# Seven quarter products for the gate and up matrices of two feed-forward layers

## The chip, the cores and the metric

The kernel runs on one core of a Trainium2 chip. The metric is device time in microseconds (us) of one execution, as the median of repeated runs. All data are float32 in memory. TensorE (PE) multiplies in a 32-bit format called fp32r, so each operand is kept as a high part (rounded to fp32r) and a low part (the rest, rounded again), and a product is made of three matmuls: high by high, high by low, low by high.

## The reference

One encoder block over 512 tokens of 1024 features:

```python
h = h + 0.5 * _swiglu(_rmsnorm(h, ffn1_norm), ffn1_w_in, ffn1_w_out)
z = _rmsnorm(h, mix_norm) @ w_in          # conv, q, k, v, r, gate
...                                       
h = h + concat([y_conv, y_gla]) @ w_out
h = h + 0.5 * _swiglu(_rmsnorm(h, ffn2_norm), ffn2_w_in, ffn2_w_out)
gate = sigmoid(_rmsnorm(h, ple_norm) @ ple_w_gate)
h = h + gate * (p @ ple_w_proj)
return _rmsnorm(h, final_norm)

def _swiglu(x, w_in, w_out):
    gate, up = jnp.split(x @ w_in, 2, axis=-1)   # 1024 -> 2816 each
    return (jax.nn.silu(gate) * up) @ w_out      # 2816 -> 1024
```

The two feed-forward layers (FFN1, FFN2) hold most of the work. Their product with `w_in` is what the change rewrites.

## The kernel before, in words

The residual is kept with features on partitions and tokens along the free axis: eight tiles `hT` of 128 features x 512 tokens. `gsplit` (L163) makes the multiplied operand `hg` from it: gain times h, as a high part (ACT) and a low part (DVE). The factor of the RMS norm, one number per token, is spread over partitions into `rsb` and multiplied in after the product.

A weight tile is fetched by `load` (L171) on SP's queue into the ring `wr` (two buffers of 128 x 2048 floats). `high` (L178) rounds it on ACT into `wh`, `low` (L188) takes the difference on DVE into `wl`; six buffers each. A block of 128 output features is made by `zblock` (L241): for each of eight k tiles of 128 input features three matmuls of 128 x 128 by 128 x 512 into one PSUM bank. PSUM has seven banks named `ps` and one named `ax`.

`ffn` (L454) walks over cuts of the 22 feature blocks (FFN1: 8, 8, 6; FFN2: 12, 10). In a cut it takes the blocks two at a time, here called a pair: gate block, up block, gate block, up block, each a `zblock`. DVE multiplies each result by `rsb`, ACT takes the silu, DVE the product, and `split` (L154) makes its high and low part (`actH`, `actL`). After a cut come its output products: for each of the eight output blocks the matmuls over the cut's feature blocks, then one DVE operation that adds half of the result to h. With the last cut the next operand and the sum of squares (`Norm`, L295) are made as well. Within `ffn`, after its first pair, the order on the engines is left to the planner (`in_order(False)`, L478); elsewhere `Ordered` (L36) keeps PE, DVE and ACT in the order in which the code is written.

The projection (from L572) begins with two weight pairs made ahead in FFN1 (`ahead`, L221), blocks pb0, pa0, pb1, pa1; the column sums of the norm stand inside pb0, the spread of the factor inside pa0 (L579, L593). The convolution's 31 taps run on DVE between the blocks (`taps`, L541), and its layer norm comes shortly before the output product (L957 to L988). The embedding stage (L1045 on) has tokens on the output partitions and ends in two half-wide products of 256 columns (L1062).

PE instructions go through the one helper of L46, so groups are told apart by tiles, not by lines.

Of the kernel before, what the change touches and what calls it, by code (L numbers as in the profile page):

```python
# [15 lines left out]
P = 128  # L16
# [15 lines left out]
FFN1_CUTS = ((0, 8), (8, 16), (16, 22))  # L32
FFN2_CUTS = ((0, 12), (12, 22))
# [29 lines left out]
def block_kernel(ctx: ExitStack, tc: tile.TileContext, a: dict, out: bass.AP):  # L63
    nc = tc.nc
    pe, dve, act = (Ordered(tc, e) for e in (nc.tensor, nc.vector, nc.scalar))
    pool = nc.gpsimd
# [50 lines left out]
    def columns(names, n, tile_name, queue):  # L117

        row = cp.tile([n, P], F32, name=tile_name + "r")
        col = cp.tile([P, n], F32, name=tile_name)  # L120
        r0 = 0
        for name, m in names:
            queue.dma_start(out=row[r0:r0 + m, :], in_=a[name][0].rearrange("(r p) -> r p", p=P))
            for c in range(m):
                vcols[name, c] = col[:, r0 + c:r0 + c + 1]
            r0 += m

        def turn():
            ps = bank()
# [32 lines left out]

    def gsplit(src, g, s):  # L163
# [6 lines left out]

    def load(src, k0, nk, c0, ncol):  # L171
        raw = wp.tile([P, 2048], F32, tag="raw", bufs=2, name=nm("wr"))
        r3 = raw[:, :nk * ncol].rearrange("p (k c) -> p k c", k=nk)
        nc.sync.dma_start(out=r3, in_=src[k0 * P:(k0 + nk) * P, c0:c0 + ncol]
                          .rearrange("(k p) c -> p k c", p=P))
        return r3
# [11 lines left out]
    def low(w):  # L188
        h3, l3, r3 = w
        dve.tensor_tensor(out=l3, in0=r3, in1=h3.bitcast(F32), op=ALU.subtract)  # L190
        return h3, l3
# [29 lines left out]
    def ahead(src, c0, ncol):  # L221


        r3 = load(src, 0, DC, c0, ncol)
        return [[low(w) for w in high4(r3[:, :, c:c + P])] for c in range(0, ncol, P)]
# [41 lines left out]
    def spread(col, copy=True):  # L267
# [7 lines left out]
        bc = tmp("bc", bufs=3)  # L275
# [59 lines left out]
    def square_x(i):  # L335
        for t in range(TB):
            junk = tmp("sq")[:, 0:X_CUTS[i + 1] - X_CUTS[i]]
            act.activation(junk, xt[t][i], AF.Square, accum_out=ssx[:, 4 * t + i:4 * t + i + 1])

    def halves(c0):  # L340

        r3 = wp.tile([P, 2048], F32, tag="raw", bufs=2, name=nm("wr"))[:, 0:D].rearrange("p (k c) -> p k c", k=DC)
        for k in range(0, DC, 4):
            def go(k=k):
                nc.sync.dma_start(out=r3[:, k:k + 4], in_=ffn1_in[k * P:(k + 4) * P, c0:c0 + P]
                                  .rearrange("(k p) c -> p k c", p=P))
# [51 lines left out]
    take(pu0, wu0, range(4, DC))  # L398
    square_x(0)
    early = (parts(raw_g1), parts(raw_u1))  # L400
# [4 lines left out]
    square_x(2)  # L405


    def load_constants():
        act.on, act.last = True, act.latest
        turn = columns(vecs[1:], nrow, "vcol", act)  # L410
        cwrow = bt(s="cwrow")[0:WIDTH, :]
        act.dma_start(out=cwrow, in_=a["conv_w"][0])
        gwu = cp.tile([2 * RANK, 2 * P], F32, name="gwu")
        for i in range(2):
            act.dma_start(out=gwu[i * RANK:(i + 1) * RANK, :], in_=a["gate_w_up"][0])
        act.on = False
        made.extend([turn, cwrow, gwu])

    def constants():
        turn, cwrow, gwu = made  # L420
        turn()
        cw = cp.tile([P, 4 * WIDTH], F32, name="cw")
        ps = bank()
# [5 lines left out]
        m1 = cp.tile([P, 4, CH], F32, name="m1")  # L429
        m2 = cp.tile([P, 4, CH], F32, name="m2")  # L430
# [14 lines left out]
    made = []  # L445

    def first_rows():
        ss = tmp("cs", 16)[:, :TB]
        dve.tensor_reduce(out=ss, in_=ssx.rearrange("p (t i) -> p t i", t=TB)[:, :, 0:3],
                          axis=mybir.AxisListType.X, op=ALU.add)  # L450
        dve.on = act.on = False
        return rsqrt_mean(ss, D, TB)

    def ffn(w_in, w_out, hg, rows, gname, cuts, early=None, meanwhile={}):  # L454
        rsb = None
        norm = Norm()
        nhg = []
        for f0, f1 in cuts:
            acts = []
            for f in range(f0, f1, 2):  # L460
                if early is None:
                    wg = weights(w_in, 0, DC, f * P, 2 * P, P)
                    wu = weights(w_in, 0, DC, DFF + f * P, 2 * P, P)
                else:
                    wg, wu = [None, early[0]], [None, early[1]]
                out = [None, None]
                if early is not None:
                    out[0] = pg0, pu0
                    early = None
                for i in range(2):  # L470
                    if out[i] is None:
                        out[i] = zblock(wg[i], hg), zblock(wu[i], hg)
                    if rsb is None:
                        pe.on, mid = True, []
                        out[1] = zblock(wg[1], hg), zblock(wu[1], hg, {
                            1: lambda: mid.append(rows()), 7: lambda: mid.append(spread(mid[0]))})
                        rsb = mid[1]
                        in_order(False)  # L478
                    pg, pu = out[i]
                    g1 = tmp("g1")  # L480
                    dve.tensor_tensor(out=g1, in0=pg, in1=rsb, op=ALU.mult)
                    s = tmp("s")
                    act.activation(s, g1, AF.Silu)
                    u1 = tmp("u1")
                    dve.tensor_tensor(out=u1, in0=pu, in1=rsb, op=ALU.mult)
                    m = tmp("m")
                    dve.tensor_tensor(out=m, in0=u1, in1=s, op=ALU.mult)
                    acts.append(split(m, "act", cvt if f - f0 < 2 else bt))
                meanwhile.get(f, int)()
            cut = 1 if f1 - f0 <= DC else 2  # L490
            nk = (f1 - f0) // cut
            for n in range(0, DC, 2):
                wa = [weights(w_out, f0 + i * nk, nk, n * P, 2 * P, P) for i in range(cut)]
                for i in range(2):
                    ps = bank()
                    for k in range(f1 - f0):
                        wh, wl = wa[k // nk][i]
                        mm3(ps, wh[:, k % nk, :], wl[:, k % nk, :], *acts[k],
                            k == 0, k == f1 - f0 - 1)
                    h = hT[n + i]  # L500
                    dve.scalar_tensor_tensor(out=h, in0=ps, scalar=0.5, in1=h,
                                             op0=ALU.mult, op1=ALU.add)
                    if f1 == cuts[-1][1]:
                        nhg.append(gsplit(h, vec(gname, n + i), "hg"))
                        norm.add(h)
        return nhg, norm
# [3 lines left out]
    meanwhile = {0: load_constants, 4: constants,  # L510
                 16: lambda: w_ahead.append(ahead(w_in, D_CONV, 2 * P)),
                 18: lambda: w_ahead.append(ahead(w_in, 0, 2 * P))}
    hg, norm = ffn(ffn1_in, a["ffn1_w_out"][0], hg, first_rows, "mix_norm", FFN1_CUTS, early, meanwhile)
# [8 lines left out]
    def pair(c0):  # L522

        r3 = load(w_in, 0, DC, c0, 2 * P)
        return [r3[:, :, i * P:(i + 1) * P] for i in range(2)]
# [53 lines left out]
    pb0 = zblock(wb[0], hg, {6: lambda: mid.append(rsqrt_mean(colsum([norm.acc]), D, TB))})  # L579
# [13 lines left out]
    pa0 = zblock(wa[0], hg, {1: lambda: mid.append(spread(mid[0]))})  # L593
    rs, rsb = mid
    low(w2a[1])
# [3 lines left out]
    pb1 = zblock(wb[1], hg)  # L599
# [45 lines left out]
    raw_v = [load(w_in, 0, 4, C_V, SEQ)]  # L645
# [67 lines left out]
    raw_r = [load(w_in, 0, 4, C_R, SEQ)]  # L713
    wv.append(high(rows4(raw_v, 2)))
# [3 lines left out]
    wv.append(high(rows4(raw_v, 3)))  # L718
# [5 lines left out]
    raw_r.append(load(w_in, 4, 4, C_R, SEQ))  # L724
# [81 lines left out]
    def outputs(t2):  # L806
# [13 lines left out]
        for t in (2 * t2, 2 * t2 + 1):  # L820
            junk = tmp("sq")
# [300 lines left out]
```

## Time and profile before

| what | us |
| --- | --- |
| median of 3 runs | 988.74 (988.57 to 989.16) |
| the profiled execution | 989.85 |
| its span, first to last instruction | 988.1 |
| PE busy in it | 972.3 |
| DVE, ACT busy in it | 533.7, 353.2 |

The span is one execution on the chip by the hardware profiler. A group of instructions is shown with its output and input tiles, shapes, count, busy time, mean length and the idle time before it. The ends of matmuls are modelled and consecutive ones overlap, so a matmul's own length (390 ns at 512 columns) is not what it costs in a row of them: that is the distance of their starts.

### The profile page before, as it was taken

What the parts mean: (1) busy time and instruction counts of PE and PEld (TensorE: products, weight loads), DVE (VectorE), ACT (ScalarE), POOL (GpSimd) and SP (SyncE); (2) the same over time, 40 slices, a digit from 0 to 9 for tenths busy, and PEclk for the clock granted to TensorE, in tenths of its full rate; (3) what the DMA queues carried; (4) which work ended last, traced back from release to release, by engine and by line L of the source; (5) the groups of instructions that cost most, each with busy time, mean ns of one, the idle gap of its engine ahead of it and who ended that gap; (6) DMA issues with size and microseconds to landing.
All of it is one profiled execution on the core that took longest, in us unless ns stands there. A gap on an engine that the chain in (4) does not pass through costs nothing.

```text
span 988.1 us, 11174 instructions
## 1 busy us (share of the span) xinstructions
PE 972.3 (98%) x4570; PEld 800.6 (81%) x4570; DVE 533.7 (54%) x756; ACT 353.2 (36%) x538; POOL 32.2 (3%) x43
## 2 busy tenths in 40 slices
PE   7999999999999999999999999999999999999996
PEld 5888888888888888788877888888888888888885
DVE  4654434444434565999986944443334454355454
ACT  5633222322223343454564633232222232234442
POOL 1000000000000000001220000000000000000000
PEclk9999999999999999999999999999999999999999
DMA  5633222322432331125654332231333222133212
GB/s 162 195 123 117 94 86 89 125 85 86 142 114 75 97 127 42 43 69 145 128 79 122 106 122 86 90 103 64 96 118 128 86 86 95 54 102 114 84 43 86
DMA packets 96505, 98.96 MB, mean 100 GB/s; under 512 B 3284, under 2 KB 89894, under 8 KB 96453
## 3 DMA queue, kind: packets, MB, share of 16 engines
q1 hardware_dynamic: 90592, 93.93, 29.5%
q0 software_dynamic: 5680, 4.20, 3.1%
q8 instruction: 36, 0.59, 0.2%
q14 instruction: 17, 0.13, 0.0%
q10 hardware_dynamic: 180, 0.12, 0.0%
HBM read 92.46 MB, written 2.10 MB: 96 GB/s over the span
## 4 chain that ended last, share of the span: by engine, by line
PE 98%; ACT 0%; DVE 0%; DMA 0%; SPq 0%; issue 0%; POOLq 0%; DVEq 0%; ACTq 0%
PE ps L46 97%; PE ax L46 1%; DMA wr<-in_ffn_w_in 0%; SPq L150 0%; DVE wl L46 0%; ACT yc L46 0%; DVE ygL L46 0%; DVE yc L46 0%; ACT ygH L46 0%; ACT hgH L46 0%; POOLq L1118 0%; ACT ycH L46 0%; ACT wa L46 0%; DVE m L46 0%; ACT h L46 0%
## 5 line engine op out<-in xcount | busy, mean ns | idle before, releaser
L46 ACT CAST wh<-wr 128x1024 fp32r<-128x1024 f32 (+2 forms) x174 | 172.1, 992 | 442.7 <-PE ps L46 419.2
L46 PE MATMUL ps<-hgH,wh 128*128 128x512 f32 x752 | 293.1, 390 | 0.0
L46 PE MATMUL ps<-hgL,wh 128*128 128x512 f32 x752 | 292.6, 389 | 0.0
L46 PE MATMUL ps<-hgH,wl 128*128 128x512 f32 x752 | 292.6, 389 | 0.0
L46 DVE TENSOR_TENSOR wl<-wr,wh 128x1024 fp32r<-128x1024 f32 (+2 forms) x169 | 193.3, 1147 | 61.4 <-ACT wh L46 61.4
L46 PEld LDWEIGHTS ps<-hgH,wh 128*128 128x128 f32 x752 | 141.2, 188 | 29.9 <-issue 0.8
L46 PEld LDWEIGHTS ps<-hgH,wl 128*128 128x128 f32 x752 | 141.1, 188 | 29.5
L46 PEld LDWEIGHTS ps<-hgL,wh 128*128 128x128 f32 x752 | 141.2, 188 | 29.3 <-DVE hgL L46 0.2
L46 PE MATMUL ps<-actL,wh 128*128 128x512 f32 x352 | 137.1, 389 | 0.0
L46 PE MATMUL ps<-actH,wl 128*128 128x512 f32 x352 | 137.0, 389 | 0.0
L46 PE MATMUL ps<-actH,wh 128*128 128x512 f32 x352 | 136.8, 389 | 0.0
L46 DVE TENSOR_TENSOR u<-ps,bc 128x512 f32<-128x512 f32 x48 | 33.1, 690 | 131.9 <-PE ps L46 131.9
L46 DVE SCALAR_TENSOR_TENSOR cv<-glu,cw,cv 128x504 f32<-128x504 f32 (+25 forms) x120 | 81.2, 728 | 0.6
L46 DVE TENSOR_TENSOR g<-ps,bc 128x512 f32<-128x512 f32 x48 | 33.1, 690 | 86.0 <-PE ps L46 83.1
L46 PEld LDWEIGHTS ps<-actL,wh 128*128 128x128 f32 x352 | 66.1, 188 | 14.0 <-DVE actL L46 0.3
L46 PEld LDWEIGHTS ps<-actH,wl 128*128 128x128 f32 x352 | 66.1, 188 | 13.8
L46 PEld LDWEIGHTS ps<-actH,wh 128*128 128x128 f32 x352 | 66.1, 188 | 13.6
L46 DVE SCALAR_TENSOR_TENSOR h<-ps,h 128x512 f32<-128x512 f32 x40 | 27.7, 692 | 88.8 <-PE ps L46 88.7
L46 PE MATMUL ps<-wh,hgH 128*128 128x512 f32 (+1 forms) x136 | 52.4, 385 | 0.0
L46 PE MATMUL ps<-wl,hgH 128*128 128x512 f32 (+1 forms) x136 | 51.7, 380 | 0.0
L46 PE MATMUL ps<-wh,hgL 128*128 128x512 f32 (+1 forms) x136 | 51.3, 377 | 0.0
L46 ACT ACTIVATE s<-g 128x512 f32<-128x512 f32 x48 | 30.3, 632 | 39.9 <-DVE g L46 35.2
(190 smaller groups left out, 767.6 us busy)
## 6 DMA issues: line engine op xcount, KB each, us to landing
wr<-in_ffn_w_in SPq DMA_DIRECT2D x42, 1024.0 KB, 5.1
wr<-in_w_in SPq DMA_DIRECT2D x10, 1024.0 KB, 5.2
wr<-in_ffn_w_out SPq DMA_DIRECT2D x12, 768.0 KB, 4.6
wr<-in_ffn_w_out SPq DMA_DIRECT2D x8, 1024.0 KB, 5.1
wr<-in_ffn_w_out SPq DMA_DIRECT2D x8, 640.0 KB, 4.1
wr<-in_w_out SPq DMA_DIRECT2D x4, 1024.0 KB
wr<-in_ple_w_gate SPq DMA_DIRECT2D x8, 512.0 KB, 3.5
wl<-wr POOLq DMA_DIRECT2D x5, 512.0 KB, 8.7
```

Source lines behind the costliest of these rows:

```text
L46: inst = call(*args, **kwargs)
```

## The change

In both layers the product with `w_in` is made in another way from the fourth pair of blocks on. Take for one pair the 256 gate features and the 256 up features, the 1024 input features in two halves of 512, and the tokens in two halves of 256. The pair's product is then a 2 x 2 by 2 x 2 product of quarters, and it is made with seven products and sums (Winograd's form) in place of eight. Products are named m1 to m7, sums of weights S1 to S4, sums of the normed input t1 to t4. A product runs over four k tiles, two blocks of 128 features and three matmuls of 256 columns. Results that several outputs share stay in a PSUM bank and are added to; ACT takes copies of it on the way (`snap`).

```diff
-FFN1_CUTS = ((0, 8), (8, 16), (16, 22))
-FFN2_CUTS = ((0, 12), (12, 22))
+HALF = SEQ // 2
+CUTS = ((0, 4), (4, 8), (8, 12), (12, 16), (16, 22))
...
+    def raw(nk, ncol):
+        return wp.tile([P, 1024], F32, tag="raw", bufs=6, name=nm("wr"))[:, :nk * ncol].rearrange(
+            "p (k c) -> p k c", k=nk)
...
-        return [[low(w) for w in high4(r3[:, :, c:c + P])] for c in range(0, ncol, P)]
+        return [[low(w, pool) for w in high4(load(src, 0, DC, c, P))] for c in range(c0, c0 + ncol, P)]
...
+    def mul(ps, w, x, first, last, ks=range(4)):
+
+        (wh, wl), k0 = w, ks[0]
+        for k in ks:
+            xh, xl = x[k]
+            for i in range(2):
+                cs = slice(i * P, (i + 1) * P)
+                o = ps[:, i * HALF:(i + 1) * HALF]
+                end = last and k == ks[-1] and i == 1
+                pe.matmul(o, wh[:, k - k0, cs], xh, start=(first and k == ks[0] and i == 0), stop=False, skip_group_check=True)
+                pe.matmul(o, wh[:, k - k0, cs], xl, start=False, stop=False, skip_group_check=True)
+                pe.matmul(o, wl[:, k - k0, cs], xh, start=False, stop=end, skip_group_check=True)
...
+    class Left:
+        def part(self, name, engine=None):
+
+            if name not in self.done:
+                self.done[name] = low(high(getattr(self, name)), engine or dve)
+            return self.done[name]
...
+            self.sum(self.s1, self.a21, self.a22, ALU.add)
+            self.sum(self.s2, self.s1, self.a11)
...
+            self.sum(self.s3, self.a11, self.a21)
...
+            self.sum(self.s4, self.a12, self.s2)
...
+        def m1(p):
+            p.x = bank()
+            mul(p.x, p.part("a11"), x.op["b11"], True, False)
+            p.a = snap(p.x, "sq", bufs=3)
+
+        def m2(p):
+            p.y = bank()
+            mul(p.y, p.part("a12"), x.op["b21"], True, True)
+
+            def gate0():
+                p.s0 = silu(plus(p.y, p.a, 0, "g1"))
+
+            return [gate0]
+
+        def m6(p):
+            mul(p.x, p.part("s2"), x.op["t2"], False, False)
+            p.u2 = snap(p.x, "u2", bufs=1)
+
+        def m7(p):
+            p.w = bank()
+            mul(p.w, p.part("s3"), x.op["t3"], True, False)
+
+        def m5(p):
+            mul(p.x, p.part("s1"), x.op["t1"], False, False)
+            p.u = plus(p.w, snap(p.x, "sq", bufs=3), 1, "u1")
+
+        def m4(p):
+            mul(p.w, p.part("a22"), x.op["t4"], False, True)
+            gated(p, p.s0, plus(p.w, p.u2, 0, "u1"), 0)
+
+        def m3(p):
+            mul(p.x, p.part("s4"), x.op["b22"], False, True)
+            s = silu(times_row(p.x, 1, "g1"))
+            return [lambda: gated(p, s, p.u, 1), lambda: act_parts(p)]
...
+            before = [(AHEAD, lambda: p.part(part))] if part else []
+            if kind in ("m1", "m2"):
+                before.append((7, lambda: p.fetch(part)))
+            elif kind == "m6":
+                before += [(9, lambda: p.fetch("a21", "a22")), (6, p.s12)]
+            elif kind in ("m7", "m3"):
+                before.append((6, p.s3_ if kind == "m7" else p.s4_))
...
+        for i in range(start, npair):
+            add("m6", i)
+            add("m7", i)
+            add("m5", i)
+            if i == end:
+                half, rest = second(cut_of[i])
+                units.append(half[0])
+            else:
+                add("m1", i + 1)
+            add("m2", i + 1)
+            units += due[:1]
+            add("m4", i)
+            add("m3", i)
+            units += due[1:2]
+            due = due[2:]
+            if i in cut_of and i < end:
+                due += second(cut_of[i])
+        units += half[1:] + rest
...
-    pb0 = zblock(wb[0], hg, {6: lambda: mid.append(rsqrt_mean(colsum([norm.acc]), D, TB))})
+    pb0 = zblock(wb[0], hg)
...
-    pa0 = zblock(wa[0], hg, {1: lambda: mid.append(spread(mid[0]))})
+    pa0 = zblock(wa[0], hg, {1: lambda: mid.append(rsqrt_mean(colsum([norm.acc]), D, TB))})
+    low(w2a[1])
+    pb1 = zblock(wb[1], hg, {1: lambda: mid.append(spread(mid[0]))})
...
+    g1_ = plain_block(w0, 0, 1, {3: lambda: mid.append(norm.rows()), 7: lambda: mid.append(spread(mid[0]))})
...
-        nc.gpsimd.dma_start(out=gfin[i], in_=a["final_norm"][i * SEQ:(i + 1) * SEQ].partition_broadcast(P))
+        nc.sync.dma_start(out=gfin[i], in_=a["final_norm"][i * SEQ:(i + 1) * SEQ].partition_broadcast(P))
```

`Left` holds one pair's weights: a11 and a12 are the gate features by the first and second half of the input features, a21 and a22 the up features. `fetch` loads one of them, `part` makes its high and low part. `Right` holds the input's quarters b11 to b22 and makes t1 to t4 from h and the gain (copies with the gain on ACT, eight subtractions on DVE, then high and low parts), in steps that are hung behind units of the plain pairs 1 and 2.

Units are run by `drive`: all of `ffn` is now written out as one list of units (a product, half of a plain block's k range, or a piece of the output product for two output blocks), and before each unit stand the preparations of later ones: a part is made `AHEAD` = 4 units before its use, the sums six, the loads seven or nine. PE, DVE and ACT keep the written order through both layers. The output products of a cut are laid between the products of the next pairs, two pieces to a pair. The first three pairs (0, 1, 2) stay plain `zblock`-like products at 512 columns: pair 0 as two blocks of gate and up ahead of the list, pairs 1 and 2 as units `h0` to `h7`.

More of the change, by code (lines that the diff above doesn't have):

```diff
@@ L161, in split, with halves @@
         return hi, lo
+    def halves(src, s):
+        hi, lo = bt(F32R, s + "H"), bt(F32R, s + "L")
+        act.copy(hi, src)
+        return hi, lo, lambda: dve.tensor_tensor(out=lo, in0=src, in1=hi.bitcast(F32), op=ALU.subtract)
     def gsplit(src, g, s):
@@ L398, in block_kernel @@
     take(pu0, wu0, range(4, DC))
+    w1 = Left(ffn1_in, 2)
+    w1.fetch("a11", "a12")
+    made = [columns(vecs[1:], nrow, "vcol", nc.sync), bt(s="cwrow")[0:WIDTH, :],
+            cp.tile([2 * RANK, 2 * P], F32, name="gwu")]
+    nc.sync.dma_start(out=made[1], in_=a["conv_w"][0])
+    for i in range(2):
+        nc.sync.dma_start(out=made[2][i * RANK:(i + 1) * RANK, :], in_=a["gate_w_up"][0])
     square_x(0)
-    early = (parts(raw_g1), parts(raw_u1))
+    early = [parts(raw_g1), parts(raw_u1)]
     for c in range(4, DC, 2):
@@ L405, in block_kernel @@
     square_x(2)
[L408 to L417, printed above, removed]
+    ss = tmp("cs", 16)[:, :TB]
+    dve.tensor_reduce(out=ss, in_=ssx.rearrange("p (t i) -> p t i", t=TB)[:, :, 0:3],
+                      axis=mybir.AxisListType.X, op=ALU.add)
+    mid = [rsqrt_mean(ss, D, TB, between=lambda: w1.part("a11"))]
+    pg1 = zblock(early[0], hg)
+    pu1 = zblock(early[1], hg, {2: lambda: w1.part("a12"), 7: lambda: mid.append(spread(mid[0]))})
+    xb = Right(hg, "ffn1_norm")
     def constants():
-        turn, cwrow, gwu = made
-        turn()
+        _, cwrow, gwu = made
         cw = cp.tile([P, 4 * WIDTH], F32, name="cw")
-        ps = bank()
+        ps = aux()
         for c in range(4):
@@ L443, in constants, with drive @@
         made[:] = cw, gwu, mean, mask, nbias
[L445 to L455, printed above, removed]
+    AHEAD = 4
+    def drive(units):
+        todo = [[] for _ in units]
+        for i, (before, _) in enumerate(units):
+            for far, f in before:
+                todo[max(i - far, 0)].append((far, i, f))
+        left = []
+        for jobs, (_, run) in zip(todo, units):
+            for *_, f in sorted(jobs, key=lambda j: (-j[0], j[1])):
+                f()
+            for f in left[:1]:
+                f()
+            new = run() or []
+            for f in left[1:]:
+                f()
+            left = new
+        for f in left:
+            f()
@@ L456, in ffn @@
+    def ffn(w_in, w_out, x, gname, given, first, rsb, hooks, plain):
         norm = Norm()
         nhg = []
[L458 to L504, printed above, removed]
-                        norm.add(h)
@@ new lines, in ffn, with row, times_row, silu @@
+        got = {}
+        npair = DFF // (2 * P)
+        end = npair - 1
+        pairs = {i: given.get(i) or Left(w_in, 2 * i) for i in range(npair)}
+        def row(i):
+            return rsb[:, i * HALF:(i + 1) * HALF].unsqueeze(1).to_broadcast([P, 2, HALF])
+        def times_row(src, i, name):
+            o = tmp(name)
+            dve.tensor_tensor(out=two(o), in0=two(src), in1=row(i), op=ALU.mult)
+            return o
+        def silu(g):
+            s = tmp("s")
+            act.activation(s, g, AF.Silu)
+            return s
@@ new lines, in plus, with scaled, gated_block @@
+        def plus(ps, t, i, name):
+            o = tmp(name)
+            dve.tensor_tensor(out=o, in0=ps, in1=t, op=ALU.add)
+            dve.tensor_tensor(out=two(o), in0=two(o), in1=row(i), op=ALU.mult)
+            return o
+        def scaled(ps, name):
+            o = tmp(name)
+            dve.tensor_tensor(out=o, in0=ps, in1=rsb, op=ALU.mult)
+            return o
+        def gated_block(p, s, u, i):
+            if not hasattr(p, "m"):
+                p.m = tmp("m", 2 * SEQ, bufs=1).rearrange("p (f c) -> p f c", f=2)
+            dve.tensor_tensor(out=p.m[:, i], in0=u, in1=s, op=ALU.mult)
@@ new lines, in snap, with gated, act_parts @@
+        def snap(ps, name, **kw):
+            o = tmp(name, **kw)
+            act.copy(o, ps)
+            return o
+        def gated(p, s, u, i):
+            if not hasattr(p, "m"):
+                p.m = tmp("m", 2 * SEQ, bufs=1).rearrange("p (f c) -> p f c", f=2)
+            dve.tensor_tensor(out=p.m[:, :, i * HALF:(i + 1) * HALF], in0=two(u), in1=two(s), op=ALU.mult)
+        def act_parts(p):
+            c = [c for c, (f0, f1) in enumerate(CUTS) if f0 <= p.f < f1][0]
+            to = cvt if c % 2 == 0 and p.f == CUTS[c][0] else bt
+            p.acts = [split(p.m[:, f, :], "act", to) for f in range(2)]
@@ new lines, in m5, with plain_unit, run, gate @@
+        def m5(p):
[8 more added lines that the diff above has]
+            return [lambda: gated(p, s, p.u, 1), lambda: act_parts(p)]
+        def plain_unit(j):
+            up, i, k = j // 4, j // 2 % 2, j % 2
+            def run(p):
+                if not j:
+                    p.g, p.s = {}, {}
+                if not k:
+                    p.x = bank()
+                ps = p.x
+                wh, wl = p.part(f"a{1 + up}{1 + k}")
+                cs = slice(i * P, (i + 1) * P)
+                for c in range(4):
+                    mm3(ps, wh[:, c, cs], wl[:, c, cs], *x.rows[4 * k + c], k == c == 0, k == 1 and c == 3)
+                if not k:
+                    return []
+                if not up:
+                    def gate():
+                        p.s[i] = silu(scaled(ps, "g1"))
+                    return [gate]
+                return [lambda: gated_block(p, p.s[i], scaled(ps, "u1"), i),
+                        lambda: act_parts(p) if i else None]
+            return run
@@ new lines, in ffn, with add @@
+        units, had = [], set()
+        def add(kind, i):
+            if 0 <= i < npair and (kind, i) not in had:
+                had.add((kind, i))
+                units.append(unit(kind, i))
+        cut_of = {f1 // 2 - 1: (f0, f1) for f0, f1 in CUTS}
+        start = 1 + len(plain)
+        due = []
+        for i in plain:
+            for j in range(8):
+                add(f"h{j}", i)
+                if j % 2:
+                    units += due[:1]
+                    due = due[1:]
+            if i in cut_of:
+                due += second(cut_of[i])
@@ new lines, in ffn @@
+        for unit_ in (("m1", start), ("m2", start), ("m1", start + 1)):
+            add(*unit_)
+        for i in range(start, npair):
[5 more added lines that the diff above has]
+                units.append(half[0])
+            else:
+                add("m1", i + 1)
+            add("m2", i + 1)
+            units += due[:1]
+            add("m4", i)
[3 more added lines that the diff above has]
+            if i in cut_of and i < end:
+                due += second(cut_of[i])
@@ L506, in ffn @@
+        units += half[1:] + rest
+        p0 = pairs[0]
+        for i in range(2):
+            s = silu(scaled(first[i][0], "g1"))
+            gated_block(p0, s, scaled(first[i][1], "u1"), i)
+        hooks.setdefault(("h0", 1), lambda *_: act_parts(p0))
+        drive(units)
         return nhg, norm
@@ L712, in block_kernel @@
     low(wv[1])
-    raw_r = [load(w_in, 0, 4, C_R, SEQ)]
-    wv.append(high(rows4(raw_v, 2)))
+    raw_r = [load(w_in, k, 2, C_R, SEQ) for k in (0, 2)]
+    wv.append(high(raw_v[2]))
     end_decay(1)
@@ L951, in block_kernel @@
     low(wo[3])
+    ffn2_in = a["ffn2_w_in"][0]
+    wf = {i: Left(ffn2_in, 2 * i) for i in range(3)}
+    w0, w1 = wf[0], wf[1]
+    w0.fetch("a11", "a12", "a21", "a22")
+    w1.fetch("a11", "a12")
     first_part(4, wo[4])
@@ L991, in block_kernel @@
     norm = Norm()
-    nhg = []
+    nhg, later, squares = [], [], []
     def wout_h(n, ps):
@@ L996, in wout_h, with lower, flush @@
         dve.tensor_tensor(out=h, in0=ps, in1=h, op=ALU.add)
-        nhg.append(gsplit(h, vec("ffn2_norm", n), "hg"))
-        norm.add(h)
+        g, hi = vec("ffn2_norm", n), bt(F32R, "hgH")
+        act.activation(hi, h, AF.Copy, scale=g)
+        sq = norm.acc if n == 0 else bt(s="sq")
+        act.activation(sq, h, AF.Square)
+        squares.append(sq)
+        flush()
+        def lower():
+            lo = bt(F32R, "hgL")
+            dve.scalar_tensor_tensor(out=lo, in0=h, scalar=g, in1=hi.bitcast(F32), op0=ALU.mult, op1=ALU.subtract)
+            nhg.append((hi, lo))
+        later.append(lower)
+    def flush():
+        for f in later:
+            f()
+        later.clear()
+    w0.part("a11")
+    w0.part("a12")
     for k in range(4):
@@ L1021, in block_kernel @@
         pT.append((hi, lo))
+    for n in range(7):
+        if n > 2:
+            part(half[n][1], half[n][0], range(0, 4), False, True)
+        wout_h(n, half[n][1])
     first_part(7, wo[7])
@@ L1024, in block_kernel, with plain_block @@
     wout_h(7, half[7][1])
-    hg, norm = ffn(a["ffn2_w_in"][0], a["ffn2_w_out"][0], nhg, norm.rows, "ple_norm", FFN2_CUTS)
+    flush()
+    w0.part("a21")
+    w0.part("a22")
+    for sq in squares[1:]:
+        dve.tensor_tensor(out=norm.acc, in0=norm.acc, in1=sq, op=ALU.add)
+    hg = nhg
+    def plain_block(p, up, i, mid={}):
+        ps = bank()
+        cs = slice(i * P, (i + 1) * P)
+        for k in range(DC):
+            if k in mid:
+                mid[k]()
+            wh, wl = p.part(f"a{1 + up}{1 + k // 4}")
+            mm3(ps, wh[:, k % 4, cs], wl[:, k % 4, cs], *hg[k], k == 0, k == DC - 1)
+        return ps
+    mid = []
+    xb = Right(hg, "ffn2_norm")
+    steps = xb.steps()
+    steps[0]()
+    g0 = plain_block(w0, 0, 0)
+    steps[1]()
+    u0 = plain_block(w0, 1, 0)
+    w1.fetch("a21", "a22")
+    w1.part("a11")
+    g1_ = plain_block(w0, 0, 1, {3: lambda: mid.append(norm.rows()), 7: lambda: mid.append(spread(mid[0]))})
+    steps[2]()
+    w1.part("a12")
+    u1_ = plain_block(w0, 1, 1)
+    steps[3]()
+    steps[4]()
+    hooks = sums_hooks(xb, ("t2", "t3", "t1", "t4"), (("h7", 1), ("h2", 2), ("h5", 2), ("m1", 3)))
+    hooks.update({("m7", 10): lambda *_: turn_p(0), ("m5", 10): lambda *_: turn_p(1)})
+    hg, norm = ffn(ffn2_in, a["ffn2_w_out"][0], xb, "ple_norm", wf, ((g0, u0), (g1_, u1_)), mid[1], hooks, (1, 2))
+    in_order(False)
+    pool.on = False
     rs = None
```

248 lines of the change are left out of this document (189 added, 59 removed).

## Prediction

> **What bounds the kernel now.** I read the page first, for the engines' shares and the chain that ended last.
>
> ```profile
> span 988.1 us, 11174 instructions
> PE 972.3 (98%) x4570; PEld 800.6 (81%) x4570; DVE 533.7 (54%) x756; ACT 353.2 (36%) x538; POOL 32.2 (3%) x43
> PEclk9999999999999999999999999999999999999999
> PE 98%; ACT 0%; DVE 0%; DMA 0%; SPq 0%; issue 0%; POOLq 0%; DVEq 0%; ACTq 0%
> ```
>
> TensorE (PE) is 98% of the chain, at full clock in every slice. So the time is the number of matmuls by their pitch (start to start), plus some 16 us without PE (988.1 - 972.3). The waits of PE name what they can of that:
>
> ```profile
> PE ps L46 <- DMA vcol1r<-in_ffn_norm: 2.3, 1, 2.3
> PE ps L46 <- DMA x<-in_x: 1.8, 2, 1.1
> PE ps L46 <- ACT ycH L46: 1.6, 1, 1.6
> PE ps L46 <- ACT wa L46: 0.9, 1, 0.9
> ```
>
> These lie at the start and in the mixing stage; none is in a feed-forward layer. The stretch table shows both kinds of matmul that the change trades. Its columns are the stretch, its length, then PE, PE weight loads, DVE, ACT and POOL busy with counts, the clock, and DMA.
>
> ```profile
> 600.00:900.00 300.00, 300.00 (x1325) 248.44 (x1324) 128.11 (x158) 85.76 (x109) 1.22 (x2) 1.00 0.29 93
> 974.48:979.75 5.27, 5.27 (x46) 5.27 (x45) 3.17 (x10) 1.75 (x6) 0.86 (x1) 1.00 0.22 85
> ```
>
> The first is the heart of the second feed-forward layer, all at 512 columns: 300 us / 1325 = 0.2264 us each. DVE is busy 43% of it, ACT 29%. The second is the tail of the embedding stage, where the kernel before already runs matmuls of 256 columns. The timeline of PE, at both ends of that stretch (46 steps lie between these two starts), gives their pitch exactly:
>
> ```profile
> 974.24 0.28 PE L46 MATMUL ps<-wh,hgL 128*128 128x256 f32 x1
> 979.75 0.28 PE L46 MATMUL ps<-wl,hgH 128*128 128x256 f32 x1
> ```
>
> (979.75 - 974.24) / 46 = 0.1198 us. That is more than half of 0.2264: two halves cost 0.2396 us, 6% over one whole. The seven products must beat this 6% with 7/8 of the work.
>
> **Matmuls, the main term.** A plain pair (two gate and two up blocks of 128 features) issues 4 x 8 x 3 = 96 matmuls of 512 columns: 96 x 0.2264 = 21.73 us. A pair in quarter products issues 7 x 4 x 2 x 3 = 168 of 256 columns: 168 x 0.1198 = 20.13 us. Each converted pair saves 1.61 us. Pairs 3 to 10 of both layers are converted, 16 in all: **-25.7 us**. The output products stay, only regrouped in five cuts. So of a theoretical eighth, 7% of a pair is left. The two pitches break even at 21.73 / 168 = 0.1294 us.
>
> The Trainium skill ("TensorE: Matmul & The Clock Gate", Back-to-back issue gap) puts the isolated gap at N/2.4 + 2.5 ns, 215.8 ns at 512 columns and 109.2 ns at 256. By it a pair would save 20.72 - 18.34 = 2.4 us and the 16 pairs 38 us. The trace's two pitches are about 11 ns above it at both sizes, and I go by the trace.
>
> **DVE and ACT, beside the matmuls.** Rows by shape, last columns busy and mean ns, then idle time:
>
> ```profile
> L46 DVE TENSOR_TENSOR wl<-wr,wh 128x1024 fp32r<-128x1024 f32 x129 | 157.2, 1222 | 39.8 <-ACT wh L46 39.8
> L46 DVE TENSOR_TENSOR u<-ps,bc 128x512 f32<-128x512 f32 x48 | 33.1, 690 | 131.9 <-PE ps L46 131.9
> L46 DVE SCALAR_TENSOR_TENSOR h<-ps,h 128x512 f32<-128x512 f32 x40 | 27.7, 692 | 88.8 <-PE ps L46 88.7
> L46 ACT CAST wh<-wr 128x1024 fp32r<-128x1024 f32 x134 | 140.3, 1051 | 338.4 <-PE ps L46 317.9 <-DMA wr<-in_ffn_w_in 8.0 <-DMA wr<-in_w_in 6.9
> L46 ACT COPY bc<-ax 128x512 f32<-128x512 f32 x3 | 1.8, 588 | 9.7 <-PE ax L46 9.7
> L46 ACT ACTIVATE s<-g 128x512 f32<-128x512 f32 x48 | 30.3, 632 | 39.9 <-DVE g L46 35.2 <-DVE u L46 4.5
> L46 ACT CAST actH<-m 128x512 fp32r<-128x512 f32 x44 | 27.4, 622 | 34.8 <-DVE m L46 34.8
> ```
>
> A plain pair costs DVE 4 lows of 1.222 and 8 operations of 0.69: 10.4 us in 21.73. A converted pair needs seven lows instead of four, four sums of weights of the same shape (S1 to S4), and 11 operations of 512 (two each after m2, m5, m4, one after m3, two gatings, two low parts): 11 x 1.222 + 11 x 0.69 = 21.0 us, against 20.13 of PE. Alone, DVE would lose. But pairs 4 to 9 each hold two pieces of output product, 2 x 24 x 0.2264 = 10.9 us of PE and 2 x 1.222 + 4 x 0.692 = 5.2 us of DVE: PE 31.0, DVE 26.2, 85%. Pair 10 holds one smaller piece (18 matmuls, 4.1 us) and stays under PE; only pair 3 has none and is over by 0.9, plus 1.7 for t4's four low parts (0.42 each, as a 256-wide DVE operation). Against that, each operand is made four units ahead of its use, three units of 2.9 us to spare. ACT has 7 x 1.051 + 3 x 0.588 + 2 x 0.632 + 2 x 0.622 = 11.6 us, 13.7 with two pieces: 44%.
>
> ```profile
> L46 DVE TENSOR_TENSOR s<-s,u 128x256 f32<-128x256 f32 x2 | 0.8, 421 | 0.4 <-ACT s L46 0.4
> ```
>
> Two handovers in a pair are shorter. m5 adds to the bank that ACT copies after m6: m7 between them gives 2.9 us for a 0.588 copy. DVE must add m7's bank to m5's copy before m4 overwrites it; in pair 3, taking DVE's queue in order from the last plain piece, DVE reaches that add some 1.3 us before m4 starts. Bounds for PE waits per layer: 0 (all covered) and 2.6 (pair 3's excess uncovered); I take 0.5, nearer the covered end since the slack is three times the excess. Two layers: **+1.0**. The sums on the normed input (11 us of DVE a layer) lie in the plain pairs, where DVE has half its time free.
>
> **Loads.** Six buffers of 1024 columns replace two of 2048, and a pair loads six tiles of 512 KB.
>
> ```profile
> wr<-in_ple_w_gate SPq DMA_DIRECT2D x8, 512.0 KB, 3.5
> SPq L174 <- DVE wl L46: 775.8, 88, 25.0
> ```
>
> At 3.5 us each that is 21 of 31 us. SP's queue is first in first out: behind a load that waits for a buffer stand all later ones. Counting from fetch to last reader, a pair's six tiles hold 46 buffer-units of the 54 there are in nine units, but for two units seven are wanted; the last fetch (a22) then waits about 1.5 units, and lands before S1's sum is due. SP waits on DVE today for up to 25 us with no PE wait behind it. I put it at 0.
>
> **Moved steps.** In FFN2 the spread of the norm follows its column sums after four k steps, not six.
>
> ```profile
> 576.61 0.95 PE L46 MATMUL ax<-ones,sqacc 128*128 128x1 f32 x8
> 580.39 0.16 DVE L46 TENSOR_TENSOR rs<-rs,rs 128x4 f32<-128x4 f32 x1
> ```
>
> From the sums' start to the norm's end is 3.94 us; the cover is now 0.8 (the sums) + 12 x 0.2264 = 3.5. PE waits **+0.4**, bounds 0 and 0.8.
>
> In the projection the spread moves one block later (into pb1), and DVE waits on it.
>
> ```profile
> 384.79 0.69 DVE L46 TENSOR_TENSOR g<-ps,bc 128x512 f32<-128x512 f32 x1
> 388.43 0.69 DVE L46 TENSOR_TENSOR u<-ps,bc 128x512 f32<-128x512 f32 x1 [2.96 <-PE ps L46]
> 393.87 0.69 DVE L46 TENSOR_TENSOR g<-ps,bc 128x512 f32<-128x512 f32 x1 [0.85 <-PE ps L46]
> 399.31 0.69 DVE L46 TENSOR_TENSOR u<-ps,bc 128x512 f32<-128x512 f32 x1 [0.31 <-PE ps L46]
> 415.96 0.69 DVE L46 TENSOR_TENSOR u<-ps,bc 128x512 f32<-128x512 f32 x1 [0.62 <-PE ps L46]
> 440.00:450.00 10.00, 10.00 (x46) 8.27 (x45) 10.00 (x15) 5.81 (x11) 1.08 (x1) 1.00 0.33 105
> ```
>
> DVE's first scaling moves one block (24 x 0.2264 = 5.4 us) later, from 384.8 to 390.2. Up to the scaling at 393.87 it has 393.87 - 384.79 - 2.96 - 0.85 = 5.3 us of work, so that one starts at 395.5, 1.6 late; the idle of 0.31 and 0.62 behind it takes this to 0.7, and from 440 DVE is full. PE would pay it at the layer norm's wait, the 1.6 of ycH above: **+0.5**, bounds 0 and 1.3. The eight low parts made ahead for the projection move from DVE to POOL, where 31 us of PE work (m3 and seven pieces) cover them.
>
> ```profile
> L753 POOL MEMSET sc<- 128x512 f32 x4 | 2.3, 849 | 0.0
> ```
>
> The nearest row of this size is a one-input 0.85; even at 3 us each, eight are 24 us: 0. The Trainium skill ("GPSIMD Engine Reference") calls two-input operations about twice as slow there as on DVE, which the cover also holds. Start and tail: earlier loads can take up to 2 us off PE's waits; the final norm's loads, now on SP ahead of the embedding weights, can add up to 3. I take 0, as neither place had a PE wait on weights over 0.9.
>
> **Sum.** -25.7 + 1.0 + 0.4 + 0.5 = -23.8. The profiled execution took 989.85 us, its span plus 1.75; that gives 966.05. The median of the runs, 988.74, is 1.1 below it: **965.0 us**.
>
> **Rivals.** *DVE paces the converted pairs.* For it: 85% busy, in strict order, and its lows waited on ACT 39.8 / 129 = 0.31 us each. If each of 13 large operations waited so, a pair with pieces needs 26.2 + 4.0 = 30.2, still under 31.0, but pair 3 runs over by 6, pair 10 by some 1 to 2. Uncovered, with a little in the six between (0.2 each), this is about 9 us in two layers: 974. *Buffers.* If a21 and a22 land later than the four units (14 us with a piece) between S1's sum and m6, PE waits in each of 16 pairs; at 1 us a pair, 981. *The loads of the stationary operand set the pace*, the case that ends slower. The rows of the weight load show 188 ns:
>
> ```profile
> L46 PEld LDWEIGHTS ps<-hgH,wh 128*128 128x128 f32 x752 | 141.2, 188 | 29.9 <-issue 0.8
> ```
>
> If a load could not begin before the last has ended, a converted pair would take 168 x 0.188 = 31.6 us, +9.9, over 16 pairs +158: 1147. It decides from a pitch of 0.1294 us, and slower than measurable begins at 0.1302. Against it: in the 256-column stretch 45 loads fit into 5.27 us, 117 ns each, though that row shows them back to back. The Trainium skill ("Perfetto Trace Analysis", Identifying the Most-Contended Engine) judges TensorE's headroom by the busy share of LDWEIGHTS rather than of matmuls, and by that 81% would rise past 100% with 1152 more loads. The 256-column stretch speaks for the rule as a warning (100% there) and against it as a bound. *The change is not what runs:* the count of PE instructions would not rise from 4570 to about 5720; then 989.
>
> **How the numbers follow.** About 0.2%, 2 us, is what a measurement of this kernel can tell from no change. Forecast (stalls up to 5 us) 0.68; DVE pacing 0.15; buffers 0.07; weight loads, or a queue blocked so that PE loses over 28 us, 0.08; no change 0.02. The low end takes no new stall (963.0) and 2 us gained at start or mixing: 961. The high end takes in DVE pacing with the tail's 3: 977. Faster 0.90, same 0.02, slower 0.08.
>
> **What would show it.** Matmuls of 256 columns at 0.120 us in long runs, about 2740 of them (16 x 168 and the tail's 48); the spans of steady pairs at 31.0 us; DVE near 85% there, PE without gaps; one PE wait of under 1 us at FFN2's spread, and a longer wait for ycH. I am wrong if the 256-column pitch is over 0.125 in the converted pairs, or if PE waits for wl, sm or wr once in every pair.

## The result, and the profile after

| | before | after |
| --- | --- | --- |
| median, us | 988.95 (988.57 to 989.93, 4 runs) | 964.65 (964.48 to 965.06, 4 runs) |
| span of the profiled execution | 988.1 | 963.3 |
| PE busy in it | 972.3 | 946.9 |

The ratio of the times is 0.9753, with a 95% interval of 0.9737 to 0.977: 24.3 us, 2.5%, faster. The forecast was 965.0, in 961 to 977.

The page of the changed kernel, its shares and its chain:

```profile
span 963.3 us, 14120 instructions
PE 946.9 (98%) x5722; PEld 835.0 (87%) x5722; DVE 731.5 (76%) x976; ACT 435.8 (45%) x678; POOL 39.9 (4%) x49
PEclk9999999999999999999999999999999999999998
PE 95%; DMA 1%; ACT 1%; DVE 1%; issue 1%; SPq 0%; POOL 0%; POOLq 0%; DVEq 0%; ACTq 0%
```

PE runs 1152 matmuls more in 25.4 us less, and it still is the chain. DVE went from 54% to 76%. The stretch table for five steady converted pairs of the second layer (first product m7 of pair 4 to that of pair 9, columns as before), then the timeline of PE at both ends of 196 steps of 256 columns:

```profile
695.60:851.00 155.40, 155.40 (x1082) 145.85 (x1082) 125.47 (x142) 63.73 (x80) 0.00 (x0) 1.00 0.32 101
```

```profile
639.75 0.28 PE L46 MATMUL ps<-hgL,wh 128*128 128x256 f32 x1
...
663.27 0.28 PE L46 MATMUL ps<-t2H,wl 128*128 128x256 f32 x1
```

A steady pair with its two pieces takes 155.4 / 5 = 31.08 us, PE never idle, DVE 81%, ACT 41%. The pitch is (663.27 - 639.75) / 196 = 0.1200 us. The waits of PE over the whole run:

```profile
PE ax L46 <- DMA vcol1r<-in_ffn_norm: 2.5, 1, 2.5
PE ps L46 <- ACT ycH L46: 1.6, 1, 1.6
PE ps L46 <- ACT wa L46: 1.2, 1, 1.2
PE ps L46 <- ACT actH L46: 1.1, 1, 1.1
...
PE ps L46 <- DVE actL L46: 0.2, 1, 0.2
```

The two new ones, for actH and actL, stand where the output products of the last cut of FFN1 first need the last pair's result, at 343 us; of the ten microseconds from 340 PE is busy for 8.63. No converted pair has a wait inside it.

### The profile page after: what moved, and what is told of

The parts are those of the page before. It is cut to its first block, busy times and chain, and to the rows that moved or that the text cites. A ratio compares the mean times of both kernels' runs of the same rounds, so it can differ in the third digit from the quotient of the medians.

```text
span 963.3 us, 14120 instructions
## 1 busy us (share of the span) xinstructions
PE 946.9 (98%) x5722; PEld 835.0 (87%) x5722; DVE 731.5 (76%) x976; ACT 435.8 (45%) x678; POOL 39.9 (4%) x49
## 4 chain that ended last, share of the span: by engine, by line
PE 95%; DMA 1%; ACT 1%; DVE 1%; issue 1%; SPq 0%; POOL 0%; POOLq 0%; DVEq 0%; ACTq 0%
PE ps L46 94%; PE ax L46 1%; DMA wr<-in_w_in 1%; DMA wr<-in_ffn_w_in 0%; DVE wl L46 0%; ACT wh L46 0%; ACT wa L46 0%; POOL wa L46 0%; SPq L149 0%; DVE g L46 0%; ACT yc L46 0%; DVE ygL L46 0%; DVE actL L46 0%; DVE yc L46 0%; ACT ygH L46 0%
## 5 line engine op out<-in xcount | busy, mean ns | idle before, releaser
L46 DVE TENSOR_TENSOR wl<-wr,wh 128x1024 fp32r<-128x1024 f32 (+1 forms) x177 | 210.7, 1202 | 52.0 <-ACT wh L46 51.6
L46 PE MATMUL ps<-hgH,wh 128*128 128x256 f32 (+1 forms) x752 | 239.1, 318 | 0.0
L46 PE MATMUL ps<-hgH,wl 128*128 128x256 f32 (+1 forms) x752 | 238.6, 317 | 0.0
L46 PE MATMUL ps<-hgL,wh 128*128 128x256 f32 (+1 forms) x752 | 238.6, 317 | 0.0
L46 ACT CAST wh<-wr 128x1024 fp32r<-128x1024 f32 (+1 forms) x182 | 184.0, 1026 | 58.9 <-PE ps L46 39.8
L46 PEld LDWEIGHTS ps<-hgH,wh 128*128 128x128 f32 x752 | 143.4, 191 | 10.7 <-issue 0.8
L46 PEld LDWEIGHTS ps<-hgH,wl 128*128 128x128 f32 x752 | 143.4, 191 | 9.5
L46 DVE SCALAR_TENSOR_TENSOR h<-ps,h 128x512 f32<-128x512 f32 x80 | 54.3, 687 | 34.5 <-PE ps L46 34.5
L46 PEld LDWEIGHTS ps<-actH,wh 128*128 128x128 f32 x352 | 66.2, 188 | 14.4 <-ACT actH L46 1.6
L46 PEld LDWEIGHTS ps<-actL,wh 128*128 128x128 f32 x352 | 66.2, 188 | 13.2 <-DVE actL L46 0.5
L46 ACT COPY sq<-ps 128x512 f32<-128x512 f32 x32 | 18.7, 586 | 67.7 <-PE ps L46 67.7
L46 ACT CAST actH<-m 128x512 fp32r<-128x512 f32 x44 | 25.5, 619 | 46.4 <-DVE m L46 46.4
```

The lines of the kernel that those rows point to most:

```text
L46: inst = call(*args, **kwargs)
```

## The experiments

The theory: PE paces the kernel before and after, the gain is the number of matmuls times their pitch, and DVE's new work is hidden. Rivals: part of the gain comes from the new order of the work; DVE already paces some pairs.

**The order without the products.**

```diff
-    ... hooks, (1, 2))
+    ... hooks, tuple(range(1, 11)))   # both layers; t1 to t4 and their steps left out
```

> The changed kernel with its whole order, ring and cuts, but all eleven pairs of both layers as plain units of 512 columns (no sums, no quarter products). Matmul theory: 16 pairs x (96 x 0.2264 - 168 x 0.1198) = 25.7 us come back, so 990.4 us, less up to 1.6 if the wait at the end of the first layer goes with the last pair's products. Rival (part of the gain comes from the new order, ring or cuts): clearly under 987.

Measured: 988.6 us (987.91 to 989.29), ratio to before 0.9994 with an interval of 0.9985 to 1.0003. New order, ring, cuts and the moved steps are worth nothing by themselves that these runs can tell; the products are worth 24 us. Its page has PE at 971.8 us busy, the changed kernel 24.9 less: 1.56 us a converted pair. PE's idle time is 15.3 against 16.4, which takes 1.1 off the gain; 24.9 - 1.1 = 23.8 is the difference of the two spans (987.1 and 963.3).

**Half of the pairs.**

```diff
-    ... hooks, (1, 2))
+    ... hooks, tuple(range(1, 7)))    # t4 split behind m1 of pair 7
```

> Pairs 1 to 6 plain, only pairs 7 to 10 of each layer in quarter products: 8 converted pairs in place of 16. Matmul theory: half of the 25.7 us is lost, 964.65 + 12.9 = 977.5 us. Rival (DVE paces some of the converted pairs, or the first ones cost more than they save): away from the middle by over 2 us.

Measured: 977.66 us (977.52 to 978.04), 13.0 over the changed kernel. The gain is linear in the pairs: PE busy 971.8, 959.3 and 946.9 us for 0, 8 and 16 converted pairs.

**The price of the half width by itself.**

```diff
-                    mm3(ps, wh[:, c, cs], wl[:, c, cs], *x.rows[4 * k + c], ...)
+                    for e in range(2):   # the same three matmuls on 256 columns each
```

> The changed kernel, with the matmuls of the plain pairs 1 and 2 of both layers each cut in two of 256 columns; same products, no other work. Theory (every matmul of 256 columns costs 0.1198, two of them 0.2396 against 0.2264): 4 pairs x 96 x 0.0132 = +5.1 us, 969.7. Rival (the 6% is special to the products of the tail, or hidden elsewhere): 964.7.

Measured: 970.16 us (969.36 to 970.24), +5.5. Over 4 x 96 = 384 matmuls cut in two, that is 14 ns each, against 13.2 from the tail of the kernel before. This is what makes seven eighths of the work into 93% of the time.

**DVE's slack.** Low parts made twice, with the same result:

```diff
+                if self.f >= 6 and name in ('s2', 'a22'):
+                    low(w, engine or dve)
```

> Two of the seven low parts of each converted pair are made twice: 2 x 1.222 us more of DVE in each of 16 pairs. DVE has slack theory: a steady pair holds 28.6 of 31.0 us, no more than +1 us, 965.6 at most. Rival (DVE paces the converted pairs now): up to 16 x 2.44 = +39 us.

Measured: 966.26 us (965.75 to 966.68), +1.6, 0.7 more than allowed, for 36 us more of DVE's busy time (767.7 against 731.5). One short wait for DVE (0.5 us) is new. The stretch table inside its steady pairs:

```profile
700.00:850.00 150.00, 150.00 (x1037) 140.41 (x1036) 133.39 (x148) 61.62 (x78) 0.00 (x0) 1.00 0.33 105
```

DVE is busy 89% there and PE has no gap.

With five of the seven made twice:

> Five of the seven low parts of each converted pair are made twice: 6.1 us more of DVE a pair. DVE has slack theory: steady pairs need 32.3 us against 31.0 of PE, pairs 3 and 10 27.2 and 28.1 against 20.1 and 24.2; the excess is 12 x 1.3 + 2 x 7.1 + 2 x 3.9 = 38 us, of which the lead of four units covers some: +15 to +38, 980 to 1003. Rival (DVE has much more room than the sum says): under 968.

Measured: 1006.75 us (1005.49 to 1006.86), +42.1 and above the expected range, ratio to before 1.0175 (1.0161 to 1.0189). So somewhere between +2 and +5 low parts a pair DVE begins to pace, and with five more the change would have lost. Three steady pairs of this run, from one wait to another:

```profile
763.67:862.57 98.90, 93.99 (x648) 87.63 (x649) 91.64 (x100) 38.06 (x49) 0.00 (x0) 1.00 0.30 96
```

A pair takes 33.0 us there, and DVE is busy 93% of it, not 100%: in 30.5 us a pair it does what the sum put at 32.3. PE waits all the same, in most pairs for ACT's copy `u`: on ACT's queue that copy stands behind casts that wait for DVE, and DVE in turn waits for ACT's casts. So DVE paces before it is full. The whole run costs more than the excess of DVE. PE's idle time rose by 30 us (1005.2 - 958.6, against 16.4), inside the bounds; its busy time rose by 11.7 as well, for the same matmuls. The stretch table shows why:

```profile
165.00:170.00 5.00, 3.82 (x32) 3.61 (x31) 3.33 (x5) 1.57 (x2) 0.00 (x0) 1.00 0.00 0
170.00:175.00 5.00, 2.32 (x11) 2.32 (x12) 4.97 (x8) 4.47 (x6) 0.00 (x0) 0.64 0.00 0
175.00:180.00 5.00, 5.00 (x31) 5.00 (x31) 4.96 (x5) 1.54 (x2) 0.00 (x0) 0.67 0.32 103
```

With a wait of 3.9 us (ending at 172.7) the granted clock falls, to 0.64 and 0.67 as the means of two stretches; in stretches of half a microsecond it reads 0.50 from 171.5 to 178. The Trainium skill ("TensorE: Matmul & The Clock Gate", Part 1) says that an idle window of about 3.4 us halves the clock until the array has been busy for as long again; the trace agrees in kind: half clock, and the full clock back some 5.5 us after PE resumes.

**The new wait at the end of FFN1.** In the timelines of ACT and DVE of the changed kernel, the number in brackets is the idle time before an instruction and its releaser:

```profile
333.67 1.14 ACT L46 CAST wa<-wr 128x512 fp32r<-128x512 f32 x2 [2.42 <-DMA wr<-in_w_in]
335.38 1.14 ACT L46 CAST wa<-wr 128x512 fp32r<-128x512 f32 x2 [0.57 <-DMA wr<-in_w_in]
336.43 0.83 ACT L46 CAST wh<-wr 128x768 fp32r<-128x768 f32 x1
```

```profile
330.41 0.69 DVE L46 TENSOR_TENSOR u<-ps,u 128x512 f32<-128x512 f32 x1 [3.21 <-PE ps L46]
331.14 1.51 DVE L46 TENSOR_TENSOR u<-u,bc 128x512 f32<-128x512 f32 x1
332.69 1.67 DVE L46 TENSOR_TENSOR m<-u,s 128x512 f32<-128x512 f32 x1
337.29 1.68 DVE L46 TENSOR_TENSOR wl<-wr,wh 128x768 fp32r<-128x768 f32 x1 [2.94 <-ACT wh L46]
338.89 0.68 DVE L46 TENSOR_TENSOR g<-ps,bc 128x512 f32<-128x512 f32 x1
```

Two things meet. ACT's queue stands behind loads of the projection's weights; behind it waits `wh` for a piece, DVE's low part of it, and behind that the scaling of the last product m3 (`g`, 338.89), whose silu and `actH` PE then needs. And three DVE operations last 1.5 to 1.7 us in place of 0.69 and 0.96 while POOL makes the low parts.

To tell the two apart, first POOL's work on DVE:

```diff
-        return [[low(w, pool) for w in high4(load(src, 0, DC, c, P))] for c in range(c0, c0 + ncol, P)]
+        return [[low(w) for w in high4(load(src, 0, DC, c, P))] for c in range(c0, c0 + ncol, P)]
```

> The eight low parts made ahead for the projection run on DVE in place of POOL, at the same place. If POOL beside DVE is what makes the wait: DVE does 8 x 0.68 = 5.5 us more but none at double length, the wait shrinks by about 1 us or goes, 963.5 to 964.5. If ACT's queue behind the loads is what makes it: the wait stays or grows by up to 2, 964.7 to 966.5.

Measured: 967.78 us (967.14 to 969.95), +3.1; the wait for actH grew from 1.1 to 2.5. Its DVE timeline, then ACT's:

```profile
331.62 0.69 DVE L46 TENSOR_TENSOR u<-u,bc 128x512 f32<-128x512 f32 x1
332.35 0.69 DVE L46 TENSOR_TENSOR m<-u,s 128x512 f32<-128x512 f32 x1
332.96 3.69 DVE L46 TENSOR_TENSOR wa<-wr,wa 128x512 fp32r<-128x512 f32 x6
...
339.82 0.96 DVE L46 TENSOR_TENSOR wl<-wr,wh 128x768 fp32r<-128x768 f32 x1
340.70 0.68 DVE L46 TENSOR_TENSOR g<-ps,bc 128x512 f32<-128x512 f32 x1
```

```profile
337.91 1.14 ACT L46 CAST wa<-wr 128x512 fp32r<-128x512 f32 x2 [4.03 <-DMA wr<-in_w_in]
338.96 0.83 ACT L46 CAST wh<-wr 128x768 fp32r<-128x768 f32 x1
```

DVE's operations are short again, and `g` is later still: ACT waits 4.03 us for a load, `wh` ends at 339.79, its low part starts at 339.82 and `g` follows. So the stretched operations by themselves are not what PE waits for; ACT's queue, which stands behind the loads, is. That does not acquit POOL. The loads wait for buffers of the ring, and a buffer comes free when its low part is made. From the chain that ended last in the changed kernel (start, length, what):

```profile
328.33 1.29 POOL wa L46
...
330.10 5.26 DMA wr<-in_w_in
...
336.52 0.75 ACT wh L46
...
338.89 0.69 DVE g L46
```

The last of the four loads starts when POOL has made the first low parts (329.62). With these on DVE they stand behind `m` (332.96 to 334.25), and the load starts at 334.27 in place of 330.10. Which link of this chain would have been enough by itself no run separates. The time is also above both expected ranges: in the profiled execution (967.21 us) the wait adds 1.4 us and PE's busy time 0.5 (947.4), and why other executions took up to 2.7 more is not shown.

Then all of it three units later (past m3 and two pieces; the expectation below counts one product more):

```diff
-                  ("m4", 10): lambda *_: w_ahead.extend([...
+                  ("q", 4): lambda *_: w_ahead.extend([...   # behind the third piece of the last cut
```

> The weights made ahead for the projection (four loads, eight high parts on ACT, eight low parts on POOL) are made two products and two pieces later, behind the third piece of the last output product. Theory (the wait of 1.4 us for actH in the first layer comes of these: ACT's queue stands behind their loads, and DVE's operations with two inputs in SBUF take over twice as long beside POOL's): the wait goes, 963.3 us. Rival (the last pair's results are simply late): 964.7.

Measured: 962.87 us (962.48 to 963.14), 1.8 under the changed kernel, and the wait for actH is gone. DVE's timeline there has `g` right behind m3:

```profile
332.08 0.95 DVE L46 TENSOR_TENSOR wl<-wr,wh 128x768 fp32r<-128x768 f32 x1
332.95 0.68 DVE L46 TENSOR_TENSOR g<-ps,bc 128x512 f32<-128x512 f32 x1
```

**POOL beside DVE, by itself.**

```diff
+                if self.f >= 6 and name == "s1":
+                    engine = pool
```

> The changed kernel, with one of the seven low parts of each converted pair (that of S1) on POOL in place of DVE, 16 in all; the same result. If POOL beside DVE only takes work off it: DVE busy falls by 16 x 1.22 = 19.5 us to 712. If the two hold each other up when both read two operands from SBUF: a POOL operation of this size lasts about 2.8 us (eight of half the size took 1.46), DVE stands still for most of it, and DVE's busy time rises by up to 16 x 1.5 = 24 us, to 732 to 756. The time stays at 964.7 within 1 in both cases, since a steady pair has 4.8 us of DVE to spare; if it rises by over 3 the slack is smaller than the sum says.

Measured: 964.39 us (964.2 to 964.7): no change. The shapes' rows:

```profile
L46 POOL TENSOR_TENSOR wl<-sm,wh 128x1024 fp32r<-128x1024 f32 x16 | 41.7, 2605 | 512.3 <-ACT wh L46 512.3
```

```profile
L46 DVE TENSOR_TENSOR u<-u,bc 128x512 f32<-128x512 f32 x32 | 30.6, 957 | 1.1
L46 DVE TENSOR_TENSOR g<-g,bc 128x512 f32<-128x512 f32 x16 | 14.0, 878 | 0.6
```

In the changed kernel the last two were:

```profile
L46 DVE TENSOR_TENSOR u<-u,bc 128x512 f32<-128x512 f32 x32 | 23.0, 718 | 1.1
L46 DVE TENSOR_TENSOR g<-g,bc 128x512 f32<-128x512 f32 x16 | 11.1, 692 | 0.6
```

DVE is busy 727.8 us where 712 would be left without any hold-up: of 19.5 us taken off it 15.8 came back, 1.0 us for each POOL operation of 2.6. (By the 1.13 us at which low parts follow one another, 18.1 were taken off and 14.4 came back, 0.9 each.) That lies between the two expectations. The Trainium skill ("SBUF — State Buffer", Who interferes with whom) says that a DVE instruction with two SBUF inputs contends with a GpSimd instruction that reads SBUF, and calls that contention an exclusive lock. The rows agree in part: operations with two inputs in SBUF grew, those with one in PSUM (`u<-ps,sq`, 0.69) did not, but DVE lost 0.9 to 1.0 us of 2.6, so for most of POOL's time it was not stopped; whether it was idle or at work on PSUM then was not taken apart.

**More pairs.** With one plain pair behind the first:

```diff
-    ... (("h7", 1), ("h2", 2), ("h5", 2), ("m1", 3)))   ...   hooks, (1, 2))
+    ... (("h7", 1), ("m1", 2), ("m2", 2), ("m1", 3)))   ...   hooks, (1,))
```

> Only pairs 0 and 1 plain, pairs 2 to 10 in quarter products: 18 converted pairs. Matmul theory: 2 x 1.61 = 3.2 us less, 961.4 us, if the sums on the normed input (11 us of DVE and ACT work) fit into pair 1. Rival (they do not fit: DVE is late for t2, t3, t1 at the first products): PE waits of several us a layer, 965 or more.

Measured: 971.8 us (971.25 to 972.57): the rival's time.

```profile
PE ps L46 <- ACT u L46: 6.5, 2, 5.6
60.00:70.00 10.00, 10.00 (x85) 10.00 (x85) 9.93 (x14) 5.98 (x10) 0.00 (x0) 1.00 0.32 107
```

In FFN1 PE waits once for 5.6 us, not for t2, t3 or t1 but for ACT's copy after m6: DVE is busy 9.93 of 10 us before it, with their low parts among its work, the scaling `g` comes late, ACT's silu waits for it and the copy stands behind the silu. The clock follows (0.72 and 0.60 in the next two stretches of 5 us). In FFN2 the same wait is 0.9. So the second layer alone, with the late weights (the run that the next expectation calls e9_ffn2_one_plain):

> The late weights of the run before last (962.87 us), and pair 2 of the second layer in quarter products too (one plain pair behind the first there, two in the first layer): 17 converted pairs. Matmul theory: -1.61 us, and back the one wait of 0.9 that the kernel with one plain pair showed in its second layer: 962.2 us. Rival (the sums on the input do not fit into one plain pair in any layer): PE waits of several us, 966 or more.

Measured: 962.63 us (962.31 to 963.12), 0.2 under the late weights alone, which is less than either's runs spread; PE's wait is 0.9. And with the splits of t2, t3 and t1 one unit or two earlier:

```diff
-    ... (("h7", 1), ("m1", 2), ("m2", 2), ("m1", 3)))
+    ... (("h6", 1), ("h7", 1), ("m1", 2), ("m1", 3)))
```

> As e9_ffn2_one_plain, with the split of t2, t3 and t1 in the second layer one unit or two earlier than there. If the wait of 0.9 us for ACT's copy after m6 comes of t3 and t1 being split just ahead of it, it goes: 961.3 us. If DVE's whole work in that stretch makes it, the wait only moves: 962.2.

Measured: 961.43 us (961.12 to 962.39), ratio to before 0.9721 (0.9708 to 0.9734); the wait is gone. That is 1.4 us under the late weights alone, for one more converted pair. This is the fastest version found, 3.2 us under the changed kernel.

## Why the prediction was right, point by point

**Matmuls.** Right in mechanism and size: -25.7 forecast, PE's busy time fell by 25.4 (972.3 to 946.9), by 24.9 with only the products taken out. The steady pair came to 31.08 us for 31.0, the pitch to 0.1200 for 0.1198. The rival of the weight loads as the pace is refuted by that pitch, at loads shown 100% busy in the same products:

```profile
640.00:663.00 23.00, 23.00 (x194) 23.00 (x193) 21.57 (x26) 11.06 (x16) 0.00 (x0) 1.00 0.37 115
```

**DVE hidden.** Right: 81% in steady pairs for 85%. The sum added full durations, but DVE's records overlap by some 0.09 us when they follow closely. The two experiments with extra low parts show that it turns between two and five of them, so the slack is shown and not only argued; but the sum took DVE as free up to 100%, and with five more PE waited at 93%. The +1.0 for waits at pair 3 did not come: no wait.

**Loads.** Right: no wait of PE for weights of a converted pair.

**FFN2's spread, +0.4.** It did not come. The chain from the sums to the norm's end is shorter than before:

```profile
559.68 0.94 PE L46 MATMUL ax<-ones,sqacc 128*128 128x1 f32 x8
560.98 1.01 POOL L46 TENSOR_TENSOR rs<-ms,negh 128x4 f32<-128x4 f32 x1 [43.16 <-DVE ms L46]
562.61 0.16 DVE L46 TENSOR_TENSOR rs<-rs,rs 128x4 f32<-128x4 f32 x1
```

It takes 3.09 us (559.68 to 562.77) in place of 3.94. The step that failed is the row it was taken from. In the kernel before, POOL's step of the norm (`rs<-ms,negh`) ran beside a DVE low part with two SBUF inputs (577.67 to 578.90):

```profile
577.89 1.86 POOL L256 TENSOR_TENSOR rs<-ms,negh 128x4 f32<-128x4 f32 x1 [48.23 <-DVE ms L46]
```

It lasted 1.86 us there and 1.01 here, where DVE waits; the 0.85 between them is all that the chain became shorter by. That the low part held POOL up is argued from these rows and was not tested.

**Projection, +0.5.** It did not come: the wait for ycH is 1.6 in both. Where DVE's delay was made up was not tried.

**POOL's low parts at 0.** This step failed. "31 us of PE work cover them" counted POOL's time against PE's, and left out what the same step puts on the other queues: eight casts on ACT's in-order queue, ahead of what the last pair needs. The casts wait for four loads, and the last load waits for a buffer that POOL's low parts give back. It cost 1.4 us of PE's time (at 343 us), 1.8 in the run that moved it. That the total came within 0.4 us of the forecast is in part luck, an exchange: 1.9 us forecast in three waits that did not come, and this one in their place; PE's time outside its matmuls rose by 0.6 us (15.8 to 16.4).

## What to carry to other kernels

Before trading wide matmuls for fewer and narrower ones, read the pitch at both widths from starts in the trace, not from durations: here 7/8 of the work gave 93% of the time. Then add up the engine that makes the operands per period, and find by doubling its work how far it is from pacing; here it paced at 93% busy. A step made ahead is free only if it stands on every queue behind what is needed first; moving it three units was worth as much as one more converted pair.

## What the runs showed of the hardware

- Two DVE operations in close succession overlap in the record: low parts of 1.22 us start 1.13 to 1.14 apart, as in the run with POOL's low parts:

```profile
171.74 1.22 DVE L46 TENSOR_TENSOR wl<-wr,wh 128x1024 fp32r<-128x1024 f32 x1
172.87 1.22 DVE L46 TENSOR_TENSOR wr<-wr,wr 128x1024 f32<-128x1024 f32 x1
```

- A long wait of PE is paid again in clock, but its length alone does not decide. In the run with five extra low parts four waits in and behind the layers (3.87, 3.93, 3.10 and 2.73 us) bring the granted clock to 0.50 for 3 to 7 us; one of 3.04 leaves it at 1.00:

```profile
305.97 0.39 PE L46 MATMUL ps<-t1H,wh 128*128 128x256 f32 x1 [3.04 <-ACT u L46]
682.34 0.39 PE L46 MATMUL ps<-hgH,wh 128*128 128x256 f32 x1 [2.73 <-DVE u L46]
```

  By an estimate from PE's busy time at that clock, the four cost some 9 of the 11.7 us that its busy time rose. In the run with one plain pair the wait of 5.6 us cost 3.3 us more (947.1, where 946.9 less two pairs of 1.56 gives 943.8).
- A two-input operation on POOL of 128 x 1024 floats took 2.6 us beside DVE's work, on DVE 1.22.
